# First modulation columns loaded alone and multiplied on TensorE, with small loads moved to ScalarE's queue

## The chip, the cores and the metric

The kernel runs on one core of a Trainium2 chip. The metric is the device time of one execution in microseconds (us). Three executions of the kernel before took 707.92, 710.3 and 712.49 us; the median is 710.3 us.

## The reference, cut to what matters

One block of a streaming encoder, for 512 tokens of width 1024 in float32. What the change touches is its very first step:

```python
mod = jax.nn.silu(c) @ w_ada[l] + b_ada[l]          # c: (1, 1024), w_ada: (1024, 6144)
sh1, sc1, g1, sh2, sc2, g2 = jnp.split(mod, 6, axis=-1)
u = rmsnorm(h, norm_mix_g[l]) * (1 + sc1) + sh1      # h = x: (512, 1024)
z = u @ w_in[l]                                      # 4296 columns, split among the branches
```

After that come a retention branch, a sparse attention branch, a gated output projection and a mixture of 16 experts; these are not edited.

## The kernel before, in words

The program is recorded first and ordered afterwards. Every call on `PE`, `ACT`, `DVE`, `POOL` or `SP` makes a record (`record`, L248), and `run` (L384) then chooses the order of all instructions of all engines with a list scheduler: it keeps a clock of its own, costs every instruction by a table (`cost`, L299), and gives a float32 matmul with one output column 117 ns (L328). Each engine executes its instructions in the order found there, and almost the whole kernel is one such run, so a change of cost or of order at the start can change the order of everything behind it. The planner keeps at most eight DMAs in flight over SP and ACT together (`lane`, L390). All instructions therefore carry the line L494 in the profile, where `run` emits them.

The stage that the change edits (L666 to L736) goes as follows.

- Loads on SP's queue (L669 to L697): the identity for the transposes, four token tiles `xs[t]` of 128 x 1024 with six small vectors between them, then four 2 MB pieces `ada[0..3]` of `w_ada` (for each of the 1024 rows 256 shift columns and 256 scale columns, tag `tADA`, three slots of 16 KB), and eight pieces `wr[0..7]` of `w_in` (128 rows by 712 columns each, 356 KB, four slots). The string in L684 gives the priority; each `wr` load holds back every load recorded after it (`R.hold`).
- RMS norm of the tokens (L703 to L707): ACT squares with a running sum, DVE, POOL and DVE scale. Then 32 PE transposes (L711) and eight ACT copies give `xnT`.
- Modulation (L715 to L731), per block `j` of 128 columns. For even `j`, DVE multiplies the eight row groups of `ada[j // 2]` by `silc[:, t]` (silu of c) and adds them up in `acc`: one TENSOR_SCALAR and seven SCALAR_TENSOR_TENSOR of 128 x 512. Two PE matmuls with a column of ones (`pm`) then sum over the partitions, for shift (s = 0) and scale (s = 1). DVE makes the pair `ab` from `pm`; ACT writes `uh[j]` in float16 and `u32`; DVE writes the remainder `ul[j]`.
- Projection (L732 to L736), per `j`: `split` cuts `wr[j]` into two float16 halves (`wh` on ACT, `wl` on DVE), and 18 PE matmuls of 512 columns (`mm3` for six column groups) add into `accs`. All later work of the first part needs the sums over the eight `j`.

PE sums and multiplies in program order: a `pm` of a later `j` stands in the same queue as the `mm3` of an earlier one.

Of the kernel before, what the change touches and what calls it, by code (L numbers as in the profile page):

```python
# [21 lines left out]
D = 1024  # L22
# [18 lines left out]
K_ID, K_TRI, K_CM, K_COS, K_SIN, K_OH, K_END = (0, 128, 256, 384, 896, 1408, 2048)  # L41
# [462 lines left out]
def block(ctx, tc, A, out):  # L504
# [9 lines left out]
    T = R.tile  # L514
    PE, ACT, DVE, POOL, SP = (Engine(R, n, e) for n, e in (
        ("PE", nc.tensor), ("ACT", nc.scalar), ("DVE", nc.vector), ("POOL", nc.gpsimd), ("SP", nc.sync)))

    def stt(o, a, s, b, op0, op1, **k):
        return DVE.scalar_tensor_tensor(o, a, s, b, op0=op0, op1=op1, **k)
# [19 lines left out]
    w_ada = A["w_ada"].rearrange("l (p t) n -> p (l t) n", p=128)  # L539
# [9 lines left out]
    def fixed(shape, dt=F32, phase=0, n=1):  # L549
        size = (2 if dt == F16 else 4) * int(np.prod(shape))  # L550
        size += -size % 32
        t = R.tag("SB", size, (place[phase], n, phase))
        place[phase] += n * size
        return T(t, shape, dt) if n == 1 else t
# [10 lines left out]
    tADA = R.tag("SB", 16 * KB, (TMP + 32 * KB, 1, 0), (Y, 1, 0), (TMP, 1, 0.5))  # L565
    tWR = R.tag("SB", 2848, (U + 32 * KB, 2, 0), (TMP + 48 * KB, 2, 0))
    tSQ = R.tag("SB", 4 * KB, (TMP + 56 * KB, 2, 0))
    tACC = R.tag("SB", 2 * KB, (TMP + 64 * KB, 1, 0), (TMP + 56 * KB, 2, 0.5))
# [40 lines left out]
    tP1 = R.tag("PS", 2 * KB, (12 * KB, 2, 0))  # L609
# [7 lines left out]
    def psa():  # L617
        return T(tA, [512])
# [4 lines left out]
    def psb():  # L623
        return T(tB, [512])

    tST, tSX = fixed([40], n=3), fixed([8], n=4)
    ident = fixed([128])
    tri = fixed([128])
    cm = fixed([128])
    ones = fixed([128])  # L630
    col = fixed([81])
    sm0 = fixed([40])
    mhalf, silc, c8, Bc, ss, rs = (sm0[:, a:b] for a, b in ((0, 1), (1, 9), (9, 17), (17, 25), (25, 29), (29, 33)))
# [32 lines left out]
    R.patience = 0  # L666

    kx = A["kconst"]
    SP.dma_start(ident, kx[:, K_ID:K_ID + 128])  # L669
    xs = []  # L670
    xnT = T(tXN, [KT, S])
    rows = T(tROW, [128])
    small_loads = [(c8, A["c"].rearrange("b (p t) -> p (b t)", p=128))]
    for o, nm in ((0, "norm_mix_g"), (8, "b_ada"), (56, "b_gate"), (72, "ret_gn_g"), (80, "dsa_kv_norm_g")):
        v = A[nm].rearrange("l (r c) -> (l r) c", c=128)
        small_loads.append((rows[o:o + v.shape[0]], v))
    for t in range(NT):
        xt = T(tXT, [D])
        SP.dma_start(xt, x_t[t])
        xs.append(xt)  # L680
        for o, v in small_loads[(0, 1, 2, 4)[t]:(1, 2, 4, 6)[t]]:
            SP.dma_start(o, v)
    ada, wr = [], []
    for c in "aaawwawwwwww":  # L684
        if c == "a":
            ra = T(tADA, [8, 2, 256])
            n = len(ada) * 256
            SP.dma_start(ra, w_ada[:, :, 0:2 * D].rearrange("p t (s n) -> p t s n", s=2)[:, :, :, n:n + 256])
            ada.append(ra)
        else:  # L690
            rw = T(tWR, [712])
            R.hold = SP.dma_start(rw[:, :712], w_in[:, len(wr), C_DKV:C_END])
            wr.append(rw)
# [14 lines left out]
    for k in range(KT):  # L708
        p = T(tP0, [512])
# [3 lines left out]
    accs = [T(tP0, [512]) for _ in range(6)]  # L713
    widths = [128, 128, 128, 128, 128, 72]
    for j in range(KT):  # L715
        if j % 2 == 0:
            ra = ada[j // 2].rearrange("p t s c -> p t (s c)")
            acc = T(tACC, [512])
            DVE.tensor_scalar(acc, ra[:, 0], silc[:, 0:1], None, op0=OP.mult)
            for t in range(1, 8):  # L720
                stt(acc, ra[:, t], silc[:, t:t + 1], acc, OP.mult, OP.add)
        pm = T(tP1, [512])
        for s in range(2):
            PE.matmul(pm[:, s:s + 1], acc[:, s * 256 + j % 2 * 128:s * 256 + j % 2 * 128 + 128], ones[:, 0:1], start=True, stop=True)
        ab = fixed([2])
        DVE.tensor_scalar(ab[:, 0:1], pm[:, 1:2], Bc[:, j:j + 1], col[:, j:j + 1], op0=OP.add, op1=OP.mult)
        DVE.tensor_scalar(ab[:, 1:2], pm[:, 0:1], col[:, 8 + j:9 + j], None, op0=OP.add)
        u32 = T(tU32, [S])
        ACT.activation(uh[:, j], xnT[:, j], AF.Identity, bias=ab[:, 1:2], scale=ab[:, 0:1])
        ACT.activation(u32, xnT[:, j], AF.Identity, bias=ab[:, 1:2], scale=ab[:, 0:1])  # L730
        DVE.tensor_sub(ul[:, j], u32, uh[:, j])  # L731
    for j in range(KT):  # L732
        wh, wl = split(wr[j], 712)
        for m in range(6):
            a, n = m * 128, widths[m]
# [7 lines left out]
    for a, b in ((0, 512), (512, 640)):  # L743
        p = T(tP1, [512])
# [12 lines left out]
    def h1():  # L757
        return T(tH1, [512], F16)
# [31 lines left out]
    for m in range(4):  # L790
        a, b = h1(), h1()
# [6 lines left out]
    p = psb()  # L798
# [9 lines left out]
    p = psb()  # L808
# [4 lines left out]
    p = psb()  # L813
# [3 lines left out]
    p = psb()  # L817
    PE.matmul(p, wkv[:, 0:2].rearrange("p a d -> p (a d)"), lat, start=True, stop=True)
    hi_lo_psum(p, 1.0, dkh, dkl)
    p = psb()  # L820
# [245 lines left out]
    for m2 in range(4):  # L1066
# [3 lines left out]
        for m in (2 * m2, 2 * m2 + 1):  # L1070
            g = gates(gw, m, 64, 1)
            p = psa()
            for k in range(4):
                a = k * 512 + (m % 4) * 128
# [91 lines left out]
    pair = T(tW8, [2, 2, D], F16, "pair")  # L1166
    hls, pick = [], T(tPK, [NT, SL], F16)
    for t in range(NT):
# [13 lines left out]
        for n in range(2):  # L1182
            p = ph[n]
            d = slice(n * 512, (n + 1) * 512)
            g = T(tT4, [512])
            o = stt(g, p, IWS, g1b[:, d], OP.mult, OP.mult)
# [227 lines left out]
    for t in range(NT):  # L1414
        h3 = h3s[t]
        for n in range(2):
            d = slice(n * 512, (n + 1) * 512)
            p = (psm, psm, psa, psf)[t]()
# [37 lines left out]
```

## Time and profile before

| | us |
|---|---|
| median of three runs | 710.3 |
| lowest and highest | 707.92, 712.49 |
| the profiled execution | 709.94 |
| its span on the core | 708.0 |
| PE busy in the span | 631.0 |
| DVE busy | 512.1 |
| ACT busy | 335.9 |

The profile shows one execution. Its span starts with the first instruction of the core and ends with the last; 1.94 us of the execution's own time lie around it. Busy times are sums over instructions and not all of them set the end. PEld is TensorE's loading of the stationary operand, an instruction of its own; a float32 matmul is two such pairs of load and multiplication in the trace. The granted clock is a share of TensorE's full 2.4 GHz; 0.50 is 1.2 GHz. The DMA share can exceed 1 where packets overlap.

### The profile page before, as it was taken

Reading aid. Unit: us, or ns where it says so; the run is one execution under the profiler, and the core shown is the slowest. Engines: PE = TensorE matmul, PEld = TensorE weight load, DVE = VectorE, ACT = ScalarE, POOL = GpSimd, SP = SyncE. Lnnn points to the kernel's source line nnn. Section 1 sums busy time; section 2 is a strip of 40 time slices with the busy share of each in tenths; the row PEclk is TensorE's granted clock in tenths of the full one; section 3 lists DMA queues with packets and bytes.
Section 4 is the critical chain, followed back from the end, with each engine's and each line's share of the span. In section 5 each row is a group of like instructions: output and inputs, shape, how many; then the busy total and the mean of one; then the engine's idle time right before and its main releaser. Section 6 shows DMA issues by size and latency. Waiting matters only on the chain. (4 is left out here: it accounts for less than half of the span.)

```text
span 708.0 us, 12292 instructions
## 1 busy us (share of the span) xinstructions
PE 631.0 (89%) x4777; PEld 371.1 (52%) x4777; DVE 512.1 (72%) x1020; ACT 335.9 (47%) x560; POOL 91.7 (13%) x80
## 2 busy tenths in 40 slices
PE   3799998999999899999799999997867889999683
PEld 2355465747566545455354444444456556777441
DVE  3998699999996668888588645578883726776426
ACT  5458632424244337775375423334446535656304
POOL 1001010211011100000000000031123320116603
PEclk9799999999999999999999999999969989999887
DMA  9998624263155376847749532943438999999745
GB/s 299 359 341 248 180 63 143 74 211 106 46 186 166 109 253 217 263 145 252 244 160 340 207 121 89 337 174 129 154 131 229 327 344 361 373 347 356 189 117 189
DMA packets 84160, 151.90 MB, mean 215 GB/s; under 512 B 9372, under 2 KB 49773, under 8 KB 83970
## 3 DMA queue, kind: packets, MB, share of 16 engines
q1 hardware_dynamic: 80690, 143.21, 61.1%
q0 software_dynamic: 3360, 7.86, 4.8%
q8 instruction: 39, 0.64, 0.4%
q14 instruction: 23, 0.19, 0.1%
q10 hardware_dynamic: 48, 0.00, 0.0%
HBM read 135.42 MB, written 14.85 MB: 212 GB/s over the span
## 5 line engine op out<-in xcount | busy, mean ns | idle before, releaser
L494 PE MATMUL banks<-arena 128*128 128x512 f16 (+9 forms) x4777 | 631.0, 295 | 64.9 <-DVE arena L494 37.9
L494 PEld LDWEIGHTS <-arena 128*128 128x128 f16 (+1 forms) x4086 | 291.3, 100 | 227.0 <-issue 33.3
L494 ACT ACTIVATE arena<-arena 128x1024 f16<-128x1024 f32 (+9 forms) x291 | 229.7, 827 | 220.4 <-DVE arena L494 98.1
L494 DVE SCALAR_TENSOR_TENSOR arena<-arena 128x1024 f16<-128x1024 f32 (+7 forms) x288 | 258.1, 918 | 61.9 <-ACT arena L494 50.0
L494 DVE SCALAR_TENSOR_TENSOR arena<-banks,arena 96x512 f32<-96x512 f32 (+11 forms) x151 | 89.2, 609 | 78.1 <-PE banks L494 50.0
L494 PEld LDWEIGHTS banks<-arena 128*128 128x128 f32 (+4 forms) x691 | 85.5, 169 | 97.0 <-issue 37.3
L494 ACT ACTIVATE arena<-banks 128x512 f32<-128x512 f32 (+9 forms) x162 | 84.2, 575 | 104.1 <-PE banks L494 103.1
L494 POOL TENSOR_TENSOR arena<-arena 128x512 f32<-128x512 f32 (+2 forms) x36 | 41.4, 1151 | 298.2 <-DVE arena L494 247.7
L494 DVE TENSOR_TENSOR arena<-arena 128x512 f16<-128x512 f32 (+6 forms) x100 | 56.1, 572 | 9.0 <-POOL arena L494 4.1
L494 ACT ACTIVATE arena<-banks,arena 128x128 f32<-128x128 f32 (+1 forms) x48 | 22.9, 531 | 41.0 <-DVE arena L494 24.9
L494 POOL DMA_INDIRECT hrow<-arena x15 | 31.7, 2110 | 37.5 <-DVE arena L494 28.6
L494 DVE TENSOR_SCALAR arena<-arena 128x1 f32<-128x1 f32 (+8 forms) x80 | 22.1, 288 | 11.7 <-ACT arena L494 5.6
L494 DVE MAX8 arena<-arena 128x8 f32<-128x256 f32 (+3 forms) x52 | 27.6, 530 | 1.4
L494 POOL DMA_INDIRECT arena<-u2row,arena x15 | 16.8, 1120 | 81.0 <-PE banks L494 65.9
L494 DVE MATCH_REPLACE8 arena<-arena 128x256 f32<-128x256 f32 (+3 forms) x56 | 27.2, 487 | 0.0
L494 POOL IOTA arena<- 128x4 int32 (+2 forms) x3 | 0.9, 297 | 193.5 <-PE banks L494 188.2
L494 DVE SCALAR_TENSOR_TENSOR arena<-arena,banks 128x512 f32<-128x512 f32 x17 | 11.6, 686 | 18.8 <-PE banks L494 17.0
L494 DVE CUSTOM_DVE_ANT_0 arena<-arena 128x128 f32<-128x128 f32 (+3 forms) x32 | 14.3, 482 | 0.0
L494 ACT ACTIVATION_READ_ACCUMULATOR arena<-arena 128x1 f32 x56 | 10.5, 188 | 0.0
L494 DVE BATCH_NORM_STATS2 arena<-banks 128x6 f32<-128x128 f32 x32 | 7.1, 284 | 3.2 <-PE banks L494 3.1
L494 DVE TENSOR_TENSOR arena<-arena,banks 128x512 f32<-128x512 f32 (+1 forms) x12 | 6.0, 512 | 3.5 <-SPq L1390 3.5
L494 DVE MATCH_VALUE_LOAD arena<-arena 128x8 f32 x56 | 5.0, 89 | 1.2
(19 smaller groups left out, 26.6 us busy)
## 6 DMA issues: line engine op xcount, KB each, us to landing
arena<-in_w_ada SPq DMA_DIRECT2D x16, 1024.0 KB
arena<-in_w_exp_gate SPq DMA_DIRECT2D x32, 512.0 KB
arena<-in_w_exp_up SPq DMA_DIRECT2D x32, 512.0 KB
arena<-in_w_exp_down SPq DMA_DIRECT2D x16, 1024.0 KB
arena<-in_w_in SPq DMA_DIRECT2D x14, 1024.0 KB
arena<-in_w_ada SPq DMA_DIRECT2D x4, 2048.0 KB
arena<-in_w_gate SPq DMA_DIRECT2D x8, 1024.0 KB
arena<-arena SPq DMA_DIRECT2D x112, 64.0 KB
```

Of the source, the lines that this page charges most:

```text
L494: o.call(*[self.real(x) for x in o.args], **{n: self.real(x) for n, x in o.kw.items()})
```

## The change

The six small loads and the identity are issued from ACT's queue; the token tiles stand alone at the head of SP's. The first 2 MB piece of `w_ada` is loaded as two pieces of 1 MB (128 shift and 128 scale columns each, rows of 512 bytes) that share one slot of `tADA`; the other three pieces stay, and the order of loads gets a new string. The modulation of `j` = 0 is made on PE alone (16 float32 matmuls with one output column, the eight row groups against `silc`); `j` = 1 on DVE from its own piece; of the pair 2 and 3 DVE adds four of the eight row groups and PE the other four, of the pair 4 and 5 six and two; the pair 6 and 7 is made as before.

```diff
-    SP.dma_start(ident, kx[:, K_ID:K_ID + 128])
-    small_loads = [(c8, A["c"].rearrange("b (p t) -> p (b t)", p=128))]
+    ACT.dma_start(ident, kx[:, K_ID:K_ID + 128])
+    ACT.dma_start(c8, A["c"].rearrange("b (p t) -> p (b t)", p=128))
     for o, nm in ((0, "norm_mix_g"), (8, "b_ada"), (56, "b_gate"), (72, "ret_gn_g"), (80, "dsa_kv_norm_g")):
         v = A[nm].rearrange("l (r c) -> (l r) c", c=128)
-        small_loads.append((rows[o:o + v.shape[0]], v))
+        ACT.dma_start(rows[o:o + v.shape[0]], v)
     for t in range(NT):
         xt = T(tXT, [D])
         SP.dma_start(xt, x_t[t])
         xs.append(xt)
-        for o, v in small_loads[(0, 1, 2, 4)[t]:(1, 2, 4, 6)[t]]:
-            SP.dma_start(o, v)
     ada, wr = [], []
-    for c in "aaawwawwwwww":
-        if c == "a":
+    sc_sh = w_ada[:, :, 0:2 * D].rearrange("p t (s n) -> p t s n", s=2)
+    for c in "01wawawwawwww":
+        if c == "0":
+            pair = T(tADA, [2, 2048])
+            ada = [pair[:, i].rearrange("p (t s n) -> p t s n", s=2, n=128) for i in range(2)]
+        if c in "01":
+            i = int(c)
+            SP.dma_start(ada[i], sc_sh[:, :, :, i * 128:(i + 1) * 128])
+        elif c == "a":
             ra = T(tADA, [8, 2, 256])
-            n = len(ada) * 256
+            n = (len(ada) - 1) * 256
...
     for j in range(KT):
-        if j % 2 == 0:
-            ra = ada[j // 2].rearrange("p t s c -> p t (s c)")
-            acc = T(tACC, [512])
+        pm = T(tP1, [512])
+        on_dve = (1, 8, 4, 6, 8)[(j + 2) // 2 if j > 1 else j]
+        if j == 0:
+            for s in range(2):
+                for t in range(8):
+                    PE.matmul(pm[:, s:s + 1], ada[0][:, t, s], silc[:, t:t + 1], start=t == 0, stop=t == 7)
+        elif j == 1 or j % 2 == 0:
+            ra, acc = ada[1 if j == 1 else (j + 2) // 2], T(tACC, [2, 128 if j == 1 else 256])
             DVE.tensor_scalar(acc, ra[:, 0], silc[:, 0:1], None, op0=OP.mult)
-            for t in range(1, 8):
+            for t in range(1, on_dve):
                 stt(acc, ra[:, t], silc[:, t:t + 1], acc, OP.mult, OP.add)
-        pm = T(tP1, [512])
-        for s in range(2):
-            PE.matmul(pm[:, s:s + 1], acc[:, s * 256 + j % 2 * 128:s * 256 + j % 2 * 128 + 128], ones[:, 0:1], start=True, stop=True)
+        for s in range(2 if j else 0):
+            c = j % 2 * 128 if j > 1 else 0
+            PE.matmul(pm[:, s:s + 1], acc[:, s, c:c + 128], ones[:, 0:1], start=True, stop=on_dve == 8)
+            for t in range(on_dve, 8):
+                PE.matmul(pm[:, s:s + 1], ra[:, t, s, c:c + 128], silc[:, t:t + 1], start=False, stop=t == 7)
```

## Rows read from the trace of the kernel before

**Rows 1.** Windows of the first 60 us; busy us (x instructions), PE clock, DMA share, GB/s
```profile
0.00:10.00 10.00, 1.76 (x7) 1.32 (x7) 2.49 (x9) 4.94 (x8) 1.75 (x13) 1.00 0.76 258
10.00:20.00 10.00, 4.66 (x27) 3.59 (x26) 5.66 (x13) 5.18 (x10) 1.10 (x2) 0.96 1.10 351
20.00:30.00 10.00, 7.22 (x22) 3.69 (x23) 9.89 (x18) 5.76 (x8) 0.00 (x0) 0.53 1.08 368
30.00:40.00 10.00, 10.00 (x52) 5.15 (x51) 9.84 (x19) 3.73 (x5) 0.00 (x0) 1.00 1.08 365
40.00:50.00 10.00, 10.00 (x52) 4.92 (x50) 9.99 (x18) 5.89 (x8) 0.00 (x0) 1.00 1.02 319
```

**Rows 2.** Timeline of the start: start us, length, engine, what, [idle before <-releaser]
```profile
10.16 1.06 ACT L494 ACTIVATE arena<-arena 128x1024 f32<-128x1024 f32 x1 [0.32 <-DMA arena<-in_x]
...
13.13 2.16 PE L494 MATMUL banks<-arena 128*128 128x128 f32 x14 [0.34 <-DVE arena L494]
...
16.14 0.49 DVE L494 TENSOR_SCALAR arena<-arena 128x512 f32<-128x512 f32 x1 [3.06 <-DMA arena<-in_w_ada]
16.66 5.47 DVE L494 SCALAR_TENSOR_TENSOR arena<-arena 128x512 f32<-128x512 f32 x7
...
22.19 1.87 PE L494 MATMUL banks<-arena 128*128 128x1 f32 x8 [6.90 <-DVE arena L494]
...
24.65 40.61 PE L494 MATMUL banks<-arena 128*128 128x512 f16 x199 [0.59 <-ACT arena L494]
...
31.66 0.97 PEld L494 LDWEIGHTS banks<-arena 128*128 128x128 f32 x8 [0.26 <-DVE arena L494]
...
39.14 0.48 DVE L494 TENSOR_SCALAR arena<-arena 128x512 f32<-128x512 f32 x1
```

**Rows 3.** PE alone in three windows of its stream: busy us (x matmuls), clock, DMA share, GB/s
```profile
24.64:29.60 4.96, 4.95 (x13) 0.52 1.10 352
...
32.70:40.30 7.60, 7.60 (x37) 1.00 1.07 371
...
41.40:50.00 8.60, 8.60 (x41) 1.00 1.01 310
```

**Rows 4.** Groups by form on PE from 24.6 to 61.7 us: count, busy us, mean ns
```profile
L494 PE MATMUL banks<-arena 128*128 128x512 f16 x120 | 30.0, 402 | 0.6 <-ACT arena L494 0.6
L494 PE MATMUL banks<-arena 128*72 128x512 f16 x24 | 6.5, 379 | 0.0
L494 PE MATMUL banks<-arena 128*128 128x1 f32 x24 | 3.0, 248 | 0.0
L494 PE MATMUL banks<-arena 32*8 32x512 f32 x2 | 1.0, 590 | 0.0
```

**Rows 5.** Timeline of SP's queue: DMA issues, start us and length
```profile
0.73 0.39 SPq L494 DMA_DIRECT2D arena<-in_c  x1
...
1.64 0.91 SPq L494 DMA_DIRECT2D arena<-in_x  x2
...
4.42 0.44 SPq L494 DMA_DIRECT2D arena<-in_x  x1
```

**Rows 6.** DMA packets of 26 to 31.5 us and of 22.3 to 25.5 us
```profile
DMA packets 1888, 1.92 MB, mean 349 GB/s; under 512 B 16, under 2 KB 1888, under 8 KB 1888
...
DMA packets 705, 1.25 MB, mean 391 GB/s; under 512 B 49, under 2 KB 388, under 8 KB 705
```

**Rows 7.** Windows of 2 us without PE work or with narrow matmuls, columns as Rows 1
```profile
4.00:6.00 2.00, 0.00 (x0) 0.00 (x0) 0.00 (x0) 0.66 (x1) 0.00 (x0) 1.00 1.06 383
...
16.00:18.00 2.00, 0.00 (x0) 0.00 (x0) 1.79 (x3) 1.53 (x4) 0.00 (x0) 1.00 1.09 346
18.00:20.00 2.00, 0.00 (x0) 0.00 (x0) 1.89 (x4) 0.00 (x0) 0.00 (x0) 0.79 1.11 351
...
524.00:526.00 2.00, 1.74 (x24) 1.73 (x24) 2.00 (x18) 1.36 (x3) 0.00 (x0) 0.50 0.00 0
```

**Rows 8.** Groups by form on DVE, 74 to 84 us: 256-element float32 operations
```profile
L494 DVE SCALAR_TENSOR_TENSOR arena<-arena 128x256 f32<-128x256 f32 x7 | 3.4, 484 | 2.5 <-ACT arena L494 1.9
```

**Rows 9.** Waits over the whole span: who for whom, us in total, times, longest us
```profile
PE banks L494 <- DVE arena L494: 37.9, 20, 8.2
```

More of the change, by code (lines that the diff above doesn't have):

```diff
@@ L680, in block @@
         xs.append(xt)
-        for o, v in small_loads[(0, 1, 2, 4)[t]:(1, 2, 4, 6)[t]]:
-            SP.dma_start(o, v)
     ada, wr = [], []
-    for c in "aaawwawwwwww":
-        if c == "a":
+    sc_sh = w_ada[:, :, 0:2 * D].rearrange("p t (s n) -> p t s n", s=2)
[7 more added lines that the diff above has]
+        elif c == "a":
             ra = T(tADA, [8, 2, 256])
-            n = len(ada) * 256
-            SP.dma_start(ra, w_ada[:, :, 0:2 * D].rearrange("p t (s n) -> p t s n", s=2)[:, :, :, n:n + 256])
+            n = (len(ada) - 1) * 256
+            SP.dma_start(ra, sc_sh[:, :, :, n:n + 256])
             ada.append(ra)
```

## The prediction

> **What bounds the kernel now.** I read the windows of the first 60 us before anything else, because the change edits only what runs there [rows 1]. The reader is to see three things. The DMA engines are full from the start (share about 1.1, 350 GB/s). DVE is full from 20 to 50 us. PE does little until 24.65 us, and from 30 us on it is busy in all of every window.
>
> The timeline says why PE starts so late [rows 2]. The last token tile is used from 10.16 us on, the transposes end at 13.13 + 2.16 = 15.29, and the first piece of `w_ada` is there at 16.14 (DVE had waited for it). Eight DVE operations take until 22.1; PE has then waited 6.90 us. Its `pm` matmuls start at 22.19 and the first projection matmul at 24.65. No gap is shown in the 40.61 us that follow.
>
> A busy PE may still wait inside, so I made the sum. Up to 61.7 us there are 120 + 24 = 144 projection matmuls (8 x 18, all of them), 24 one-column instructions and 2 others [rows 4]. The first 13 take 4.96 us at a granted clock of 0.52; at 1.00, 37 take 7.60 us and 41 take 8.60, 0.21 us each [rows 3]. The one-column ones come eight at a time in 0.97 us, 0.121 each [rows 2]. So 24.65 + 4.96 + 131 x 0.21 + 24 x 0.121 + 1.0 = 61.0 us, which is where they end. PE is therefore the bound from 24.65 to 61 us: DVE is as full, but just ahead of it. What the stage is worth is set by two numbers, when the stream starts and how much work PE has in it.
>
> **The change part by part.**
>
> Loads. Before, the token tiles are issued at 1.64 us (two), later, and at 4.42 us, with small loads between [rows 5]. Alone on SP, the first goes where SP's first load goes now, about 0.9 us sooner. After that the stream is full either way, so the whole stream moves by 0.9 us at most and by nothing at least (seven small loads still share the DMA engines, and ACT must issue them). I take 0.9, because the DMA engines are full from 4 us on, long before anything waits for `w_ada` [rows 7]. The bytes do not change. The Trainium skill speaks against more: DMA: Bandwidth & Descriptors, section "Issuing engines are not separate DMA queues", says that loads started from several engines run on the same 16 DMA engines and that only the issue time is saved. By that rule the 0.9 us, which is issue time, is all there is.
>
> Packets. The two halves of the first piece come in rows of 512 bytes, which no row shows at volume. Rows of 1 KB ran 1888 packets in 5.5 us on 16 engines, 46.6 ns for 1017 bytes; a mixture with longer rows ran 705 in 3.2 us, 72.6 ns for 1773 bytes [rows 6]. The line through both gives 29 ns for 512 bytes, a quarter more per byte. The nearest bounds are 23.3 ns (nothing per packet) and 46.6 ns (all per packet); I take 29. A half then takes 3.75 us where 2 MB took 16.14 - 10.16 = 5.98 [rows 2], and lands at 10.16 - 0.9 + 3.75 = 13.0 us (12.2 to 15.3), before the transposes end at 15.29 - 0.9 = 14.4. So it seldom decides. The Trainium skill puts the smallest row for full rate at 512 bytes (the same page, section "Specifications"). By that rule a half would land at 12.3 us; the sum stays, and no run here shows which is right.
>
> The first block on PE. 16 float32 matmuls are 32 instructions, as two matmuls for each `j` show as four. At full clock 32 x 0.121 = 3.9 us; at half clock 8 took 1.87 us [rows 2], 0.234 each, 7.5 us. The granted clock was still 1.00 from 16 to 18 us, with PE idle since 15.3, and fell between 18 and 20 [rows 7]. The block comes right behind the transposes, so I take the full clock for it and keep 7.5 as the other end. It ends at 14.4 + 3.9 = 18.3. From the end of the first block's sums to the first projection matmul it is 24.65 - (22.19 + 4 x 0.234) = 1.5 us now; I keep that. `wr[0]` follows the two halves, lands at 13.0 + 3.75 + 1.0 = 17.8 and is split in time. The stream starts at 19.8, **4.85 us sooner**.
>
> DVE. The seven operations behind the first take 5.47 us and the first 0.49 [rows 2]: 6.0 us for each of four pairs, 24 us. After the change `j` = 1 costs eight 256-element operations at 0.484 [rows 8], 3.9 us, and the pairs 3.0, 4.5 and 6.0: 17.4. The 6.6 us saved lie beside PE's stream and count as nothing; without that cover (PE waiting for DVE) they would be a gain. What matters is that DVE stays ahead: the last pair's chain starts at 39.14 now [rows 2], comes about as early after, and is needed by PE at 54.
>
> PE's added work. For the pair 2 and 3, four row groups, two sums and two blocks are 16 matmuls, 32 instructions; for 4 and 5, 16 instructions; the four of `j` = 1, which stood ahead of the stream, are now in it. 52 x 0.121 = **6.3 us more in the stream**. They stand in PE's queue ahead of the projection matmuls of the same and later `j`, and no other engine waits while they run except through these. Bounds: nothing, if the loads of weights hid behind 512-column matmuls, and 0.234 each at half clock (12.2 us). I take 0.121, because the eight in the stream of now took just that between such matmuls.
>
> The cold start of the stream. 13 matmuls took 4.96 us where 13 x 0.21 = 2.7 would do. I take the same after.
>
> Sum: -4.85 + 6.3 = +1.45 us at the end of the stage. All later parts need these sums, so I carry it through. The profiled execution took 709.94 us (span 708.0 and 1.94 around it), 0.36 under the median of 710.3; 709.94 + 1.45 = **711.4 us**. The gain at the front is given back inside the stream.
>
> **The rivals.**
>
> *The clock stays up.* PE no longer stops for 6.90 us ahead of the stream. If its one-column work keeps the clock at 1.00, the 13 first matmuls take 2.7 us and not 4.96: 711.4 - 2.3 = 709.1 us. Against it: from 524 to 526 us PE was busy 1.74 of 2 us with 24 narrow matmuls and the clock stayed at 0.50 [rows 7]. TensorE: Matmul & The Clock Gate of the Trainium skill, section "Why this matters for your kernels", advises against idle gaps between bursts of matmuls, since the clock then drops; by that rule this rival would win. The trace agrees on the drop behind the gap at 15.3 us, and leaves open what one-column work does.
>
> *The clock falls early*, the rival on the slower side. If it falls as PE begins the first block, 32 instructions take 7.5 us: the stream starts at 23.4, and the sum is -1.25 + 6.3 = +5.05, 715.0 us. It decides when the clock is at 0.50 before the first block is half done. For it: the fall came by itself in the same region, and the transposes now end sooner. Against: the work follows without a gap.
>
> *The order behind changes.* One planner orders everything, and its table holds a one-column float32 matmul for 117 ns where the trace shows two instructions of 0.121 us. With other times at the front it may place later matmuls otherwise, on PE, which keeps its order. The price is that of one long wait won or lost: PE waited for DVE 20 times, 37.9 us in all, 8.2 at the longest [rows 9]. That gives 711.4 - 8.2 = 703 or, with a gain of DVE's relief beside it, a little less, and 719.6 on the other side. Nothing in the trace says which.
>
> **How the numbers follow.** Main case 0.40 (711.4); clock stays up 0.14 (709.1); clock falls early 0.16 (715.0); another order with a gain of more than 1% 0.16 (about 702), with a loss of more than 1% 0.14 (about 719). About 1% is what a measurement of this kernel can tell from no change, 7.1 us: from 703.2 to 717.4. The first three cases lie inside, so: faster 0.16, same 0.70, slower 0.14. The range reaches to the order cases until about 2 in 10 are out: 702.5 to 718. The likeliest case's own range is 708 to 716: loads moved by nothing (+0.9), one-column work partly hidden (-3), clock partly down (+3.6).
>
> **What would show each step.** The transposes should end near 14.4 us, a block of 32 one-column instructions should follow with hardly a gap, and the stream should start near 19.8. The granted clock around 18 to 20 us decides between the first three cases. One-column instructions inside the stream should number 76 (24 + 52) and take 0.12 each; the 144 projection matmuls should end near 62.5. PE should show no wait for `wr[1]`, which now comes behind a 2 MB piece. The prediction is wrong if the stream shows gaps, if the one-column work takes much less than 0.12 us each, or if the differences of the two traces lie behind 70 us.

## The result and the profile after

The changed kernel takes 717.6 us (median of 19 runs, 711.42 to 724.42), beside 710.81 us for the kernel before (19 runs on the same chip, 707.64 to 716.97). The two medians lie 6.8 us apart. The ratio, from which one execution of after in a slower state (724.42 us) is left out, is 1.0069 [1.0044, 1.0094], with its 95% interval in brackets. By it after is slower by 4.9 us (3.1 to 6.7): within 1%, on the slow side. The profiled execution of after took 711.63 us, the low end of its runs, with a span of 709.8 us. From the page of after, the span and the busy time of each engine:

```profile
span 709.8 us, 12441 instructions
PE 640.0 (90%) x4853; PEld 379.5 (53%) x4853; DVE 505.8 (71%) x1014; ACT 336.0 (47%) x560; POOL 90.4 (13%) x80
```

DVE does 6.3 us less than before and PE is busy 9.0 us longer. The timeline of after answers to [rows 2] (start us, length, engine, what, idle before and its releaser):

```profile
4.84 0.21 ACT L494 ACTIVATE arena<-arena 128x8 f32<-128x8 f32 x1 [0.38 <-DMA arena<-in_c]
6.69 4.71 SPq L494 DMA_DIRECT2D arena<-in_w_ada  x2
9.68 1.06 ACT L494 ACTIVATE arena<-arena 128x1024 f32<-128x1024 f32 x1 [0.92 <-DMA arena<-in_x]
15.18 4.57 PE L494 MATMUL banks<-arena 128*128 128x1 f32 x40 [1.33 <-DMA arena<-in_w_ada]
19.08 0.35 DVE L494 TENSOR_SCALAR arena<-arena 128x256 f32<-128x256 f32 x1 [6.17 <-DMA arena<-in_w_ada]
21.75 47.42 PE L494 MATMUL banks<-arena 128*128 128x512 f16 x230 [2.00 <-ACT arena L494]
```

The last token tile is used 0.5 us sooner than before, not 0.9. The first half of the first piece is used at 15.18 us, and PE had waited for it. The stream starts at 21.75 us, 2.9 us sooner than in [rows 2]. To see what is left of that at the end of the stage I take two landmarks: the first eviction of a projection sum on ACT, and the first small sum on POOL behind the stage. The timeline of before:

```profile
59.73 1.06 ACT L494 ACTIVATE arena<-banks 128x512 f16<-128x512 f32 x2
68.17 1.93 POOL L494 TENSOR_TENSOR arena<-arena 128x4 f32<-128x4 f32 x1 [55.88 <-DVE arena L494]
```

and that of after:

```profile
65.14 0.58 ACT L494 ACTIVATE arena<-banks 128x512 f16<-128x512 f32 x1
73.65 2.03 POOL L494 TENSOR_TENSOR arena<-arena 128x4 f32<-128x4 f32 x1 [61.52 <-DVE arena L494]
```

A stream that starts 2.9 us sooner ends 5.4 us later. Windows of after inside it (columns as in [rows 1]):

```profile
16.00:18.00 2.00, 2.00 (x21) 2.00 (x20) 0.00 (x0) 1.37 (x3) 0.00 (x0) 1.00 0.97 273
18.00:20.00 2.00, 1.75 (x16) 1.66 (x15) 0.85 (x3) 0.00 (x0) 0.00 (x0) 0.88 1.05 365
28.00:30.00 2.00, 2.00 (x7) 0.82 (x6) 2.00 (x4) 1.65 (x3) 0.00 (x0) 0.56 1.09 353
34.00:36.00 2.00, 2.00 (x20) 2.00 (x20) 0.35 (x2) 1.52 (x2) 0.00 (x0) 1.00 1.09 352
36.00:38.00 2.00, 2.00 (x9) 0.78 (x9) 1.00 (x3) 1.38 (x2) 0.00 (x0) 0.65 1.10 349
38.00:40.00 2.00, 2.00 (x6) 0.83 (x5) 1.79 (x4) 0.83 (x2) 0.00 (x0) 0.50 1.10 361
40.00:42.00 2.00, 2.00 (x10) 0.87 (x9) 1.97 (x4) 0.00 (x0) 0.00 (x0) 1.00 1.03 389
```

The clock is at 1.00 in both windows inside the one-column blocks (16 to 18 and 34 to 36 us, PE busy in all of them) and falls to 0.50 at the end of each block or right behind it (19.5 and 36.6 us). The second fall, 36.6 to 40 us, has no counterpart in [rows 3]. Behind the stage the lag of after wanders: +5.5 us at 68 us, about +9 at 175 to 198, 7 to 8 at 208 to 250, +3.8 at 439 to 530, +1.5 at 696 (single executions of each kernel). That is why the rest of the work compares the landmark as well as the end.

### The profile page after: what moved, and what is told of

Its sections match the earlier page's. It is cut to its first block, busy times and chain, and to the rows that moved or that the text cites. A ratio compares the mean times of both kernels' runs of the same rounds, so it can differ in the third digit from the quotient of the medians.

```text
span 709.8 us, 12441 instructions
## 1 busy us (share of the span) xinstructions
PE 640.0 (90%) x4853; PEld 379.5 (53%) x4853; DVE 505.8 (71%) x1014; ACT 336.0 (47%) x560; POOL 90.4 (13%) x80
## 3 DMA queue, kind: packets, MB, share of 16 engines
q0 software_dynamic: 3360, 7.86, 4.8%
## 5 line engine op out<-in xcount | busy, mean ns | idle before, releaser
L494 PE MATMUL banks<-arena 128*128 128x96 f16 (+8 forms) x4853 | 640.0, 294 | 56.4 <-DVE arena L494 30.9
L494 DVE SCALAR_TENSOR_TENSOR arena<-arena 128x1024 f16<-128x1024 f32 (+7 forms) x282 | 252.2, 916 | 56.5 <-ACT arena L494 45.5
L494 PEld LDWEIGHTS banks<-arena 128*128 128x128 f32 (+4 forms) x767 | 93.7, 170 | 93.8 <-issue 35.8
L494 ACT ACTIVATE arena<-banks 128x512 f32<-128x512 f32 (+10 forms) x162 | 84.8, 569 | 88.8 <-PE banks L494 87.5
L494 POOL TENSOR_TENSOR arena<-arena 128x512 f32<-128x512 f32 (+2 forms) x36 | 39.9, 1111 | 308.2 <-DVE arena L494 276.9
L494 POOL DMA_INDIRECT hrow<-arena x15 | 29.2, 1944 | 36.5 <-DVE arena L494 24.3
L494 DVE TENSOR_SCALAR arena<-arena 128x1 f32<-128x1 f32 (+9 forms) x80 | 22.0, 286 | 14.6 <-DMA arena<-in_w_ada 6.2
L494 POOL DMA_INDIRECT arena<-u2row,arena x15 | 18.3, 1218 | 80.4 <-PE banks L494 51.2
L494 DVE SCALAR_TENSOR_TENSOR arena<-arena,banks 128x512 f32<-128x512 f32 x17 | 11.6, 686 | 19.8 <-PE banks L494 17.6
L494 ACT ACTIVATION_READ_ACCUMULATOR arena<-arena 128x1 f32 x56 | 10.5, 188 | 0.0
L494 DVE TENSOR_SCALAR arena<-banks,arena 128x1 f32<-128x1 f32 x16 | 3.2, 242 | 8.7 <-PE banks L494 8.6
```

The lines of the kernel that those rows point to most:

```text
L494: o.call(*[self.real(x) for x in o.args], **{n: self.real(x) for n, x in o.kw.items()})
```

## The experiments

"Landmark" is the POOL sum above, from one profiled execution.

**The same kernel once more** (no edit), to see how much one execution differs from another.

> The changed kernel once more, for a second profile. Stage theory (the loss is PE's added one-column work and the clock that falls behind it): the stream starts at 21.8 us again, the one-column block near 31 us takes 4.6 us again, a second fall of the granted clock shows within 6 us of it, and the first projection sum is evicted near 65 us. Order theory (the loss arises behind 70 us): these times hold too, and the falls of the clock behind 200 us come at the same places as in the first profile. If the falls come elsewhere, they belong to the execution and not to the kernel.

It took 709.64 us. Its timeline:

```profile
15.47 6.06 PE L494 MATMUL banks<-arena 128*128 128x1 f32 x40 [1.52 <-DMA arena<-in_w_ada]
22.93 47.01 PE L494 MATMUL banks<-arena 128*128 128x512 f16 x225 [1.40 <-ACT arena L494]
75.28 2.04 POOL L494 TENSOR_TENSOR arena<-arena 128x4 f32<-128x4 f32 x1 [63.06 <-DVE arena L494]
```

The first block took 6.06 us instead of 4.57: the clock fell inside it, not behind it. The landmark is 1.6 us later, and yet the whole execution 2 us shorter. A total of one execution says nothing on a stage of 5 us.

**The small loads back on SP's queue**, the rest as in after:

```diff
-    ACT.dma_start(ident, kx[:, K_ID:K_ID + 128])
-    ACT.dma_start(c8, A["c"].rearrange("b (p t) -> p (b t)", p=128))
+    SP.dma_start(ident, kx[:, K_ID:K_ID + 128])
+    small_loads = [(c8, A["c"].rearrange("b (p t) -> p (b t)", p=128))]
...
+        for o, v in small_loads[(0, 1, 2, 4)[t]:(1, 2, 4, 6)[t]]:
+            SP.dma_start(o, v)
```

> The changed kernel with its small loads back on SP's queue between the token tiles. Late-load theory (on ACT's queue the small loads land late, and SP waits for them before it may issue the last token tile and the halves): the silu waits for c until about 2.4 us and not 4.8, the first half lands at about 13.5 to 14.5 us and not 15.2, the stream starts 1 us sooner or more, and the median is 1 to 2 us below that of the changed kernel (ratio to before 1.005). Row-length theory (the late halves come from rows of 512 bytes alone): the stream starts within 0.5 us of 21.8, and the ratio stays at 1.007.

726.02 us (720.03 to 731.38), ratio 1.0184 [1.0131, 1.0236]. Its timeline:

```profile
2.44 0.21 ACT L494 ACTIVATE arena<-arena 128x8 f32<-128x8 f32 x1 [0.42 <-DMA arena<-in_c]
17.02 0.35 DVE L494 TENSOR_SCALAR arena<-arena 128x256 f32<-128x256 f32 x1 [4.05 <-DMA arena<-in_w_ada]
22.37 7.73 PE L494 MATMUL banks<-arena 128*128 128x512 f16 x25 [2.80 <-ACT arena L494]
```

`c` is there at 2.44 us instead of 4.84, the second half at 17.02 instead of 19.08: both loads land 2 us sooner. Still the stream starts no sooner, so the expected gain of 1 us missed. In this execution the clock fell inside the first block, at 17.6 us, and the wait for ACT ahead of the stream grew from 2.00 to 2.80 us. ACT had been idle for 2.54 us up to 20.11, then made `uh[0]` and `u32`, and `wh[0]`, which PE needs as well, only behind them:

```profile
21.54 0.78 ACT L494 ACTIVATE arena<-arena 128x712 f16<-128x712 f32 x1
```

In after `wh[0]` is the first of the three, as its load lands at 20.08 us. The landmark is at 74.18, as in after. By the two ratios, though, this kernel is 1.15%, 8.2 us, slower than after. With stages that end alike, that comes from behind the stage; from what, the next runs had to show.

**The shared pairs back on DVE**, the first block still on PE:

```diff
-        on_dve = (1, 8, 4, 6, 8)[(j + 2) // 2 if j > 1 else j]
+        on_dve = (1, 8, 8, 8, 8)[(j + 2) // 2 if j > 1 else j]
```

> The changed kernel with all eight row groups of the pairs 2 to 7 added on DVE; only block 0 stays on PE. Stage theory: 48 one-column instructions less in the stream (5.6 us) and no second fall of the clock (1.7 us), so the first projection sum is evicted near 58 us and not 65, and the median is 5 to 7 us below that of the changed kernel, at 0.998 of before or less. DVE theory (PE would now wait for DVE, which has 7.5 us more to do): the eviction comes later than 61 us and the ratio is 1.002 to 1.006. Order theory: the eviction is sooner, the end is not.

712.71 us, 1.0016 [0.9981, 1.005]. The eviction came at 65.85 us and not near 58, so the expectation from the sum missed. The timeline says why:

```profile
15.55 7.86 PE L494 MATMUL banks<-arena 128*128 128x1 f32 x40 [1.93 <-DMA arena<-in_w_ada]
24.82 12.67 PE L494 MATMUL banks<-arena 128*128 128x512 f16 x40 [1.40 <-ACT arena L494]
38.05 1.05 PE L494 MATMUL banks<-arena 128*128 128x1 f32 x8 [0.56 <-DVE arena L494]
```

In this execution the first block ran at half clock in nearly all of it (7.86 us), the stream started no sooner than before, and PE then waited for DVE, which has the pairs whole again. The expected absence of a second fall missed too: the clock is at 0.50 from 40.2 to 43.6 us, with no block of 40 in the stream, behind eight one-column instructions and two waits of PE (0.56 us for DVE, 0.96 for ACT). Of the five profiles of kernels without PE's share of the pairs, three show such a fall. Landmark and total disagree once more: the landmark is as late as in after, the total some 4 us lower (1.0016 against 1.0069; the two intervals just overlap).

**Both edits**: small loads on SP and the pairs on DVE.

> Both of the edits before this: small loads on SP's queue, and the pairs 2 to 7 all on DVE; what is left of the change is block 0 on PE from its own half piece. Stage theory with the late-load theory: stream from about 20.5 us, first eviction near 57 us (before: 59.7), ratio 0.995 to 0.998. If the early start is worth nothing, 1.000.

708.85 us (703.42 to 712.26) beside 711.21 for the kernel before: 0.9965 [0.9936, 0.9994]. This beats both kernels, by a margin that barely excludes none. Its landmark, 74.28, is 6.1 us later than that of before; the gain doesn't show in the stage that was edited. That one execution is a late one, though: its one-column matmuls stand 0.21 us apart in all of the first block, the spacing at half clock, where the same kernel in its staged form (below) started the stream 4.4 us sooner.

**The order behind the stage held fixed.** Three of these kernels have the landmark of after and totals 17 us apart, so the order has to be taken out. In all kernels named "staged" the list scheduler is run once at the end of the stage and started anew for the rest, from the same state; the instructions behind the stage then stand in the same order on every engine, whatever the stage is:

```diff
     p_dkv, p_iq, p_ik = accs[0], accs[1:5], accs[5]
+    kept = [uh, ul, ohb, *accs]
+    for v in kept:
+        R.keep(v)
+    R.run()
+    R.clock, R.work = {"PE": 90000.0}, {}
...
```

Applied to before and to after:

> The kernel before, planned in two pieces: the planner finishes the first stage (through the projection of the eight blocks), is then set to one fixed clock, and plans the rest from there. The four kernels of this call so have the same order of instructions behind the stage on every engine, and differ in the stage alone. Stage theory and order theory agree on this one: the stage as before (stream from 24.7 us, first eviction of a projection sum near 60 us), and a total that may lie some us above 711 because nothing of the next part is mixed into the stage. It is the base for the other three.

> The changed kernel planned in the same two pieces. Stage theory: the 5.4 us by which the first eviction came later in the profile stay through to the end, so the median is 4 to 7 us above that of the staged kernel before (ratio 1.006 to 1.010). Order theory: the stage is not what sets the end; with one order behind it the two medians differ by less than 2 us.

749.17 us (1.0542 [1.0491, 1.0593]) and 755.24 us (1.0639 [1.0595, 1.0683]). The cut itself costs 38 us (749.17 against 711.04 for the kernel before in the same series); it is in all staged kernels alike. The timelines at the landmark, first of the staged kernel before:

```profile
68.40 1.02 POOL L494 TENSOR_TENSOR arena<-arena 128x4 f32<-128x4 f32 x1 [55.19 <-DVE arena L494]
```

then of the staged kernel after:

```profile
76.97 1.02 POOL L494 TENSOR_TENSOR arena<-arena 128x4 f32<-128x4 f32 x1 [64.63 <-DVE arena L494]
```

The stage of after ends 8.6 us later here (its first block took 7.37 us in this execution), and the median is 6.1 us higher. From the landmark on, PE, DVE, ACT and POOL have the same instructions in the same order in all the staged traces. With one order, a lag made in the stage arrives at the end.

**The parts of the change, staged.** Small loads on SP:

> The changed kernel with the small loads on SP's queue, staged. Unstaged it took 726 us, although its stage ended within 1 us of the changed kernel's. Order theory of that: with the common order it is within 2 us of the staged changed kernel. If the loads on SP cost something of their own, it stays 8 us or more above it.

754.38 us, 1.0621 [1.0581, 1.066]; landmark 75.32. So ScalarE's queue shows 1.65 us at the landmark, no more than two executions of after differ by, and 0.9 in the median, which the intervals don't separate: its cost at the end is not shown. And the 726 us of the unstaged kernel are gone: with the order held it is no slower than the staged after. Then the pairs on DVE as well:

> Block 0 on PE from its half piece, small loads on SP, the pairs on DVE, planned in two pieces like the staged kernels. Unstaged this kernel was at 0.9965 of before although the first rstd of the latent (a landmark just behind the stage) came 6.1 us later than before. Order theory: with the common order behind the stage it is 4 us or more slower than the staged kernel before (753 or more, ratio 1.060 or more), so the unstaged gain lay in the order. If the stage itself gains, it is at or below 749.

748.42 us, 1.0532 [1.0476, 1.0588]; its timeline:

```profile
68.83 1.02 POOL L494 TENSOR_TENSOR arena<-arena 128x4 f32<-128x4 f32 x1 [56.24 <-DVE arena L494]
```

Taking PE's share of the pairs away moves the landmark from 75.32 to 68.83 (6.5 us) and the median by 6.0 us. This is the cost of that part, measured alone, with the falls of the clock that it brings; about 1 us of the landmark's 6.5 is an earlier stream (21.29 us against 22.32), as the clock fell behind the first block in this execution and inside it in the other. The kernel doesn't get clearly below the staged kernel before, though the stream starts at 21.29 us: the waits of PE (us in total, times, longest) from 20 to 66 us in this kernel are

```profile
PE banks L494 <- DVE arena L494: 4.2, 4, 1.8
PE banks L494 <- ACT arena L494: 3.8, 2, 2.8
```

where the same kernel with the share on PE (the staged one with small loads on SP) waits only once for long:

```profile
PE banks L494 <- ACT arena L494: 2.8, 1, 2.8
PE banks L494 <- DVE arena L494: 0.3, 1, 0.3
```

**The clock alone.** The staged after with 64 equal output columns instead of one in every matmul of the modulation: the same instructions in the same number, with more columns. The first column of each block is used as before.

```diff
-                    PE.matmul(pm[:, s:s + 1], ada[0][:, t, s], silc[:, t:t + 1], start=t == 0, stop=t == 7)
+                    PE.matmul(pm[:, s * 64:s * 64 + 64], ada[0][:, t, s], silc[:, t:t + 1].to_broadcast([128, 64]), start=t == 0, stop=t == 7)
...
```

> The staged changed kernel with 64 equal output columns instead of one in every float32 matmul of the modulation (the vector is broadcast; one of the 64 columns is read). Count, order of operands and loads of weights stay. Clock theory (PE runs at half clock because one-column work counts as none): the granted clock does not fall at 18 us nor near 37 us, the stream starts at full clock, and the first eviction comes 3 to 5 us sooner than in the staged changed kernel. Length theory (only the number of instructions counts): the falls stay, or the wider matmuls take longer themselves, and the eviction comes as late or later.

Windows of the staged after:

```profile
16.00:18.00 2.00, 2.00 (x17) 2.00 (x15) 0.00 (x0) 1.58 (x4) 0.00 (x0) 0.74 0.93 193
18.00:20.00 2.00, 2.00 (x11) 2.00 (x11) 0.30 (x1) 0.00 (x0) 0.00 (x0) 0.50 1.06 378
36.00:38.00 2.00, 2.00 (x16) 1.60 (x16) 0.59 (x3) 1.34 (x3) 0.00 (x0) 0.86 1.10 348
38.00:40.00 2.00, 2.00 (x6) 0.62 (x5) 1.01 (x2) 2.00 (x3) 0.00 (x0) 0.50 1.11 358
```

and of the same kernel with 64 columns:

```profile
16.00:18.00 2.00, 2.00 (x21) 2.00 (x20) 0.00 (x0) 1.60 (x4) 0.00 (x0) 1.00 1.03 317
18.00:20.00 2.00, 2.00 (x20) 2.00 (x19) 0.78 (x2) 0.00 (x0) 0.00 (x0) 1.00 1.08 364
36.00:38.00 2.00, 2.00 (x12) 0.98 (x12) 1.40 (x4) 1.35 (x3) 0.00 (x0) 1.00 1.10 349
38.00:40.00 2.00, 2.00 (x11) 0.94 (x10) 1.72 (x3) 0.90 (x2) 0.00 (x0) 1.00 1.09 366
```

PE is busy in all of each of these windows, with one column or with 64. With 64 the clock stays at 1.00 through both blocks and behind the second, where with one column it falls three times (17.0, 37.4 and 51.1 us). It still falls to 0.50 from 22.0 to 25.4 us, behind PE's wait of 1.64 us ahead of the stream, so the expected start of the stream at full clock missed. The wider instructions take no longer (4.57 us in after):

```profile
15.62 4.58 PE L494 MATMUL banks<-arena 128*128 128x64 f32 x40 [1.59 <-ACT arena L494]
```

So in this pair the falls in and behind the two blocks go with the single column and not with a gap. The landmark is at 72.61 instead of 76.97, 4.4 us sooner, where two executions of after differ by 1.6. Not all of that need be the clock: the planner reckons with the number of columns, and PE and DVE have part of the stage's work in another order. The medians, 753.96 (1.0603 [1.0559, 1.0647]) and 755.24, are too close to be told apart: that these 4.4 us arrive at the end is not shown.

**The halves without PE.** Small loads on SP, `j` = 0 on DVE from its own half like `j` = 1, all pairs on DVE; PE makes the old sums only.

```diff
-        on_dve = (1, 8, 4, 6, 8)[(j + 2) // 2 if j > 1 else j]
+        on_dve = (8, 8, 8, 8, 8)[(j + 2) // 2 if j > 1 else j]
...
-        elif j == 1 or j % 2 == 0:
+        if j <= 1 or j % 2 == 0:
...
```

> The same without staging. If the stage gains and the order behind costs nothing, 706 to 708 us (ratio 0.994 to 0.997). The order theory allows anything between 0.985 and 1.015, whatever the stage does.

708.7 us, 0.9967 [0.993, 1.0004]: not separable from the kernel before. The timeline:

```profile
13.46 0.35 DVE L494 TENSOR_SCALAR arena<-arena 128x256 f32<-128x256 f32 x1 [0.63 <-DMA arena<-in_w_ada]
17.05 0.35 DVE L494 TENSOR_SCALAR arena<-arena 128x256 f32<-128x256 f32 x1 [0.62 <-DMA arena<-in_w_ada]
21.07 11.25 PE L494 MATMUL banks<-arena 128*128 128x512 f16 x40 [1.82 <-ACT arena L494]
33.05 1.05 PE L494 MATMUL banks<-arena 128*128 128x1 f32 x8 [0.74 <-DVE arena L494]
```

and windows of the same stretch:

```profile
24.00:34.00 10.00, 9.26 (x40) 4.33 (x41) 9.43 (x17) 3.58 (x5) 0.00 (x0) 0.85 1.08 363
34.00:44.00 10.00, 8.39 (x43) 4.25 (x44) 9.93 (x21) 5.70 (x8) 0.00 (x0) 1.00 1.04 334
```

The stream starts 3.6 us sooner than before with no work added to PE. But DVE now has no time left (9.9 of 10 us), PE waits for it (8.39 of 10 us busy), and the landmark, 69.05, is no sooner than before. Staged:

> The half pieces alone, staged: small loads on SP, both halves multiplied on DVE as eight 256-element operations each, no modulation work on PE beyond the two sums for each block. It takes the whole of the PE work away and keeps the early landing. Stage theory: the first half lands at 13.5 us, eight operations take 3.9 us, the stream starts at 19 to 20 us (staged before: 24.95), PE has no more work than before, and the landmark comes 2 to 5 us sooner than in the staged kernel before (64 to 66 us; 68.4 there), with a total of 744 to 747. DVE theory (DVE, 1.9 us busier with the halves, becomes the bound): the stream starts as early but shows waits for DVE, and the landmark stays within 1.5 us of 68.4.

749.89 us, 1.0581 [1.0515, 1.0647], beside 749.17 for the staged kernel before, and the landmark at 69.13 against 68.40, as the theory of DVE as the bound had it: with the order held, no gain. So the 2 us by which the two unstaged kernels without PE's share are below the kernel before are not made in the stage. They come with the order, or are none; which instructions of it, stays open.

## Why the prediction was right and where it failed

The class and the range held: 717.6 us lies in 702.5 to 718, 0.4 us below its end. That is owed to the width that the cases with another order gave the range: the likeliest case's own range, 708 to 716, missed it. The mechanism of that case, a gain at the front that PE's work inside the stream gives back, was right; its size was not, +1.45 us where +4.9 (3.1 to 6.7) were measured. Along its own steps:

**Loads: failed.** "I take 0.9" was the upper bound; the last token tile came 0.5 us sooner, and the half came later than forecast by 2.2. The wait of SP's queue for the identity in after (us in total, times, longest), and the issue of the fourth token tile:

```profile
SPq L494 <- DMA arena<-in_kconst: 4.2, 1, 4.2
6.31 0.33 SPq L494 DMA_DIRECT2D arena<-in_x  x1
```

SP issued three tiles by 2.1 us and then waited 4.2 us for the identity, which had gone to the other queue: the three tiles and five loads from ACT held the planner's eight places. The fourth tile was issued at 6.31 us, where before it was issued at 4.42 [rows 5], and the first half right behind it, at 6.69. The DMA engines then weren't full. The window of 8 to 10 us in after (columns as in [rows 1]), and below it that of the kernel with the small loads on SP:

```profile
8.00:10.00 2.00, 1.62 (x8) 1.41 (x9) 1.33 (x6) 1.08 (x3) 0.55 (x1) 1.00 0.83 295
8.00:10.00 2.00, 1.57 (x7) 1.23 (x7) 1.25 (x4) 1.26 (x3) 0.56 (x1) 1.00 1.04 348
```

The step had the shared DMA engines in its lower bound; what it left out are the planner's eight places, and "full either way" did not hold. The half landed at 15.18 us and not at 13.0; with the loads on SP it lands at 13.46, so 1.7 of these 2.2 us are ScalarE's queue. The Trainium skill's DMA: Bandwidth & Descriptors, section "Issuing engines are not separate DMA queues", says that loads of all issuing engines interleave on the same DMA engines and that only issue time is saved. The trace agrees that no more is saved, and shows a loss beside it: the last tile came 0.5 us sooner, `c` 2.4 us later than with the loads on SP.

**Packets: right.** 29 ns for 512 bytes on 16 engines is 282 GB/s. The DMA view of the kernel with the small loads on SP, from 10.5 to 16 us, where nearly all packets are 512-byte rows:

```profile
DMA packets 3110, 1.61 MB, mean 293 GB/s; under 512 B 28, under 2 KB 3095, under 8 KB 3110
```

In the kernel with both halves on DVE they are used from 13.46 and 17.05 us on, 3.59 us apart, where 3.75 was forecast. Rows of 1 KB ran at 349 GB/s [rows 6]. The Trainium skill's DMA: Bandwidth & Descriptors, section "Specifications", has full rate from 512 bytes on; these two rates don't bear that out.

**First block on PE: right in one execution.** In after 40 instructions (the 32 and eight of the transposes) took 4.57 us, 0.114 each, against 0.121; in other executions and kernels 6.06, 7.37 and 7.86. Both ends of the bound occur, according to where the clock falls; 4.57 and 6.06 are of the same program. Choosing one end was the mistake; the bound itself held.

**Tail of 1.5 us: short.** 2.0 us in after, where `wr[0]` landed at 20.08 us and not at 17.8, and 2.8 where the half came sooner; in each the wait is for ACT. With the 0.8 us of the later landing and 0.7 of the longer block this puts the stream at 21.75 instead of 19.8.

**PE's added work: right.** The groups by form in after from 21.7 to 66.5 us, as in [rows 4]:

```profile
L494 PE MATMUL banks<-arena 128*128 128x512 f16 x120 | 32.6, 421 | 2.0 <-ACT arena L494 2.0
L494 PE MATMUL banks<-arena 128*128 128x1 f32 x76 | 9.2, 252 | 0.0
L494 PE MATMUL banks<-arena 128*72 128x512 f16 x23 | 7.5, 424 | 0.0
```

76 one-column instructions took 9.2 us, 0.121 each. The 40 in a row took 4.65 us, 0.116 each: 52 x 0.116 = 6.0 us added.

**"I take the same after", the cold start: failed.** Before, 4.96 us at half clock; after, 8.0 us from 21.75 on. A projection matmul takes 0.43 us at half clock and 0.21 at 1.00, so a stretch at half clock loses half its length and this is 1.5 us dearer. And behind the 40 one-column instructions inside the stream the clock fell a second time, 3.4 us at 0.50 (36.6 to 40.0), worth 1.7 us. The prediction listed the clock as a rival on either side, but only for the start of the stream. Its sign against a clock that stays up, the 24 narrow matmuls of [rows 7], was misread: 22 of them have 96 output columns and two have 16, in float16 and with 0.7 us of waiting between them, so they say nothing of one column.

**DVE's saved time counted as nothing: right as far as PE is the bound**, and it hid how near DVE is. Without PE's share DVE sets the pace and the sooner start is lost (above).

The sum with the measured terms: -2.9 + 6.0 + 1.5 + 1.7 - 1.0 (the two other matmuls, which moved from inside the stream to 66.87 us) = +5.3, beside 5.4 measured at the eviction. Of the rivals, *the clock falls early* gave 715.0 us and comes nearest; in the executions where the first block took 7.4 to 7.9 us it is just what happened, and in that of the profile the clock fell behind the block and again later. *The clock stays up* is refuted. TensorE: Matmul & The Clock Gate of the Trainium skill, section "Why this matters for your kernels", warns of idle gaps. The second fall in after comes in a stream that shows no gap for 47.42 us, so a gap is not the only way to it. *The order behind changes* did not decide here: with the order held the change costs 6.1 us, without 4.9. But the size of this rival was right: 8.2 us lie between two kernels whose stages end alike, and are gone when the order is held.

Not tried: ScalarE's queue as the only change to the kernel before, the 64 columns with the order inside the stage held as well, and any one piece of the later order put back.

## What to carry to other kernels

Work moved from one full engine to another is paid at the receiver's price: the pairs' share, four row groups of one pair and two of another, cost 6 us on PE, and taking it back with a sooner start of the stream gained nothing, since then DVE was full. An engine with room would be the better receiver; that was not tried here. Where one planner orders the whole program, hold the order behind the edited stage before judging the edit; unstaged totals here lay 8 us and more apart for kernels whose stages end alike. Count matmuls with one column twice, once as instructions and once for the clock behind them. With 64 equal columns the instructions here took no longer and the clock held; a gain from that at the end is not shown.

## What the runs showed of the hardware beyond the forecast

- In all five profiles with 40 one-column float32 matmuls and loads in a row inside the stream, PE busy throughout, the granted clock fell from 1.00 to 0.50 inside that block or within 1 us behind it (at 34.4 to 38.7 us); with 64 columns, in one profile, it stayed at 1.00. Where exactly it falls differs between executions of one program (4.57 and 6.06 us for the same block).
- A small load moved to the other queue came later, not sooner: `c`, issued at 0.74 us in both, was used at 4.84 us from ACT's queue, where SP issued tiles beside it, and at 2.44 us from SP's, ahead of every tile.
- Rows of 512 bytes ran at 293 GB/s where rows of 1 KB ran at 349.
- A clock of 1.00 in a window can stand for no record: in the profile of the kernel with both edits the record begins at 30.45 us and the windows before it show 1.00, while 46 one-column and transpose loads from 13.22 us took 9.57 us, 0.21 each. In after_again the spacing of one-column matmuls goes from 0.11 to 0.21 us where the recorded clock goes from 1.00 to 0.50, so 0.21 is the half clock.
